# Down projection of a gated MLP by Strassen's scheme in seven of its eight groups, on one core

## Chip, cores and metric

The kernel runs on one core of a Trainium2 chip. The metric is device time in microseconds (us) for one launch, the median of the runs shown. TensorE is written PE, its weight loads PEld, VectorE DVE, ScalarE ACT, GpSimd POOL, and SyncE, which issues the transfers, SP.

## What is computed

One layer of a decoder trunk on 512 tokens of width 1024 in float32. A mixing stage (four token mixers, gates, an output projection) gives a residual `h`; then comes an MLP with a norm on both sides. The change touches only the MLP and where its buffers lie:

```python
h = h + rms_norm(mix, norm_mix_post[l])
u = rms_norm(h, norm_mlp_pre[l])
hid = jnp.square(jax.nn.relu(jnp.einsum("btd,df->btf", u, w_up[l])))   # 1024 -> 4096
m = jnp.einsum("btf,fd->btd", hid, w_down[l])                          # 4096 -> 1024
h = h + rms_norm(m, norm_mlp_post[l])
```

## The kernel before

**Three matmuls for one.** Every float32 operand x is split into a high part, a rounded copy that ACT writes (L140), and a low part, x minus the high part, that DVE writes (L141). A product is then three matmuls, high by high, high by low and low by high, issued by `mm3` (L181 to L183), each with a moving operand of 512 columns. A weight unit is 128x1024: `load` brings it into one of three `raw` buffers (L135, on SP), `prep` splits it into one of six pairs `whi`, `wlo`, and `unit` hands units out in the order of use, preparing four ahead.

**The MLP.** The 4096 hidden features are done in 8 groups (`NG`) of 512, that is 4 blocks (`GF`) of 128. `up_group` makes the hidden values of a group in two pairs of blocks: a pair is 48 matmuls (2 blocks, 8 blocks of the inner width, 3 products) into two PSUM banks of 512, and `up_out` then applies relu on ACT (L850), a square on DVE (L851) and the split. The first group, `up_first`, runs in two column halves of 256, so that it can start when only half the tokens are normalised; the last two token tiles are transposed between (L807). `down_group` multiplies: for each of 4 token tiles and each half of the 1024 outputs, 12 matmuls of 512 columns (4 blocks, 3 products) into one PSUM bank, added to the sum `macc` in SBUF by DVE (L914; in group 0 ACT copies it, L912). So a group is 96 matmuls up and 96 down. The order is up 0, up 1, down 0, up 2, down 1 and so on. In the last group every finished row of tokens is squared and summed on ACT (L738), scaled by the gain (L888), multiplied by its norm factor and added to the residual `h1`, which stayed in SBUF (L892), and stored (L894).

A down group's core:

```python
 904            for pi, (a, b) in enumerate(pieces):
 905                ps = sm_bank()[:, : b - a]
 906                for j in range(GF):
 907                    wh, wl = us[j]
 908                    mm3(ps, hh[j // 2][:, j % 2, t * P : t * P + P], hl[j // 2][:, j % 2, t * P : t * P + P],
 909                        wh[:, a:b], wl[:, a:b], j == 0, j == GF - 1)
 910                m = macc[t][:, a:b]
 911                if g == 0:
 912                    act.activation(m, ps, AF.Copy)
 913                    continue
 914                dve.tensor_tensor(m, m, ps, ALU.add)
```

**What sets the order.** The program is written as above; a scheduler with its own estimate of durations places the instructions on each engine, so on PE the matmuls of an up pair and of a down group can be interleaved. Each engine then runs its list strictly in order, and waits for the others at semaphores. Buffers of a pool are reused in turn, so a write to a buffer waits for its last reader.

Of the kernel before, what the change touches and what calls it, by code (L numbers as in the profile page):

```python
# [49 lines left out]
def tile_hybrid_trunk(ctx: ExitStack, tc: tile.TileContext, xT, xn, wts, par, bd, cst, msk, gains, out):  # L50
# [5 lines left out]
    yp = ctx.enter_context(tc.tile_pool(name="yp", bufs=8))  # L56
    ap_ = ctx.enter_context(tc.tile_pool(name="ap", bufs=4))
    tp = ctx.enter_context(tc.tile_pool(name="tp", bufs=10))
# [3 lines left out]
    mp = ctx.enter_context(tc.tile_pool(name="mp", bufs=4, space=bass.MemoryType.PSUM))  # L62
    qp = ctx.enter_context(tc.tile_pool(name="qp", bufs=4, space=bass.MemoryType.PSUM))
    npool = ctx.enter_context(tc.tile_pool(name="np", bufs=2))

# [33 lines left out]
    bd_h = cp.tile([P, 6, P], F32R, name="bd_h")  # L99
    bd_l = cp.tile([P, 6, P], F32R, name="bd_l")  # L100
    msk_s = cp.tile([P, len(MASKED), 64], U8, name="msk_s")
    rstd_bc = cp.tile([P, T], F32, name="rstd_bc")
    sbd = cp.tile([P, 3, 2, P], F32, name="sbd")
# [14 lines left out]

    NU = wts.shape[0]
# [23 lines left out]
    def prep(n):  # L143
        while Wt.n_prep < min(n, NU):
            i = Wt.n_prep
# [17 lines left out]
            Wt.hl[i] = (hi, lo)  # L163
            Wt.n_prep += 1
            load(i + 3)

# [88 lines left out]
    ssq = cp.tile([P, NT], F32, name="ssq")  # L255
# [91 lines left out]
    lbt = cp.tile([P, 8], F32, name="lbt")  # L347
# [35 lines left out]
    vz = cp.tile([P, NT, 2, 192], F32, name="vz")  # L383
# [42 lines left out]
    def lru_steps():  # L426
# [28 lines left out]
        spt = cp.tile([P, 16], F32, name="spt")  # L455
# [49 lines left out]
    def hgrn_steps():  # L505
# [39 lines left out]
        ds_ = cp.tile([P, 4 * NT], F32, name="ds_")  # L545
# [84 lines left out]
        ms = cp.tile([P, 16], F32, name="ms")  # L630
        rs = cp.tile([P, 16], F32, name="rs")
# [83 lines left out]
    load_gain(1)  # L715
    h1 = []
# [117 lines left out]

    def up_mm(bk, w, h, a, b):
        wh, wl = w
        for kk in range(4):
            k = 4 * h + kk
            for c in range(2):
                o = kk * W + c * P  # L840
                mm3(bk[c][:, a:b], wh[:, o : o + P], wl[:, o : o + P],
                    U(u2h, k, a, b), U(u2l, k, a, b), k == 0, k == NK - 1)

    def hid_tiles():
        return [[yp.tile([P, 2, T], F32R, tag="y", name=nm("hid")) for _ in range(2)] for _ in range(2)]

    def up_out(hid, s, bk):
# [6 lines left out]
    def up_first():  # L854
        hid = hid_tiles()
        bks = [[mm_bank(), mm_bank()] for _ in range(2)]
        us = {}
        for h in range(2):
            for s in range(2):
                us[s, h] = unit()  # L860
                up_mm(bks[s], us[s, h], h, 0, 256)
                if (s, h) in ((1, 0), (0, 1)):
                    t = 2 if h == 0 else 3
                    tb = trans(t, sm_bank)
                    put(t, 0, tb[0])
                    put(t, 1, tb[1])
        for s in range(2):
            for h in range(2):
                up_mm(bks[s], us[s, h], h, 256, T)
            up_out(hid, s, bks[s])  # L870
        return hid

    def up_group():
        hid = hid_tiles()
        for s in range(2):
            bk = [mm_bank(), mm_bank()]
            for h in range(2):
                up_mm(bk, unit(), h, 0, T)
            up_out(hid, s, bk)
        return hid  # L880

    load_gain(2)
    macc = [ap_.tile([P, D], F32, tag="acc", name=nm("macc")) for _ in range(NT)]

    mgs = {}

    def gain(t, a, b):
        dve.tensor_tensor(mgs[t][:, a:b], macc[t][:, a:b], gbc[2][:, a:b], ALU.mult)  # L888

    def half(t, r, a, b):  # L890
        m = mgs[t][:, a:b]
        dve.scalar_tensor_tensor(m, m, r, h1[t][:, a:b], ALU.mult, ALU.add)  # L892
        eng = nc.scalar if t == NT - 1 and a == T else nc.sync
        eng.dma_start(out[t * P : t * P + P, a:b], m)  # L894

    def down_group(g, hid):
        hh, hl = hid
        us = [unit() for _ in range(GF)]
        last = g == NG - 1
        for t in range(NT):  # L900
            pieces = ((0, T), (T, 2 * T))
            if last and t == NT - 1:
                pieces = ((0, T), (T, T + 256), (T + 256, D))
            for pi, (a, b) in enumerate(pieces):
                ps = sm_bank()[:, : b - a]
                for j in range(GF):
                    wh, wl = us[j]
                    mm3(ps, hh[j // 2][:, j % 2, t * P : t * P + P], hl[j // 2][:, j % 2, t * P : t * P + P],
                        wh[:, a:b], wl[:, a:b], j == 0, j == GF - 1)
                m = macc[t][:, a:b]  # L910
                if g == 0:
                    act.activation(m, ps, AF.Copy)  # L912
                    continue
                dve.tensor_tensor(m, m, ps, ALU.add)  # L914
                if last:
                    sq_only(m, 4 + t, pi)
                    if pi < 1 or t < NT - 1:
                        v = sq_tot(4 + t, pi, stat[:, t, 6:7] if pi == 0 else v, 3 + pi)
                    if pi == 0:
                        mgs[t] = t_tile()[:, :D]  # L920
                    if t < NT - 1 or pi < 2:
                        gain(t, a, b)
            if last:
                if t == NT - 1:
                    v = sq_tot(4 + t, 1, v, 4)
                    v = sq_tot(4 + t, 2, v, 5)
                r = row_rstd(v, 4 + t, (lambda: gain(t, T + 256, D)) if t == NT - 1 else None)
                if t == NT - 1:
                    half(t, r, 0, T)
                    half(t, r, T, T + 256)  # L930
                    half(t, r, T + 256, D)
                else:
                    for a, b in ((0, T), (T, D)):
                        half(t, r, a, b)

    ahead[0] = 2
    hid = up_first()
    ahead[0] = 4
    for t in range(NT):
        row_eps(t)  # L940
    for g in range(1, NG):
        nh = up_group()
        down_group(g - 1, hid)
        hid = nh
    down_group(NG - 1, hid)


def _layout(inp):
# [38 lines left out]
    for g in range(1, NG + 1):  # L987
        if g < NG:
            upg(g)
        for j in range(GF):  # L990
            units.append(wd[GF * (g - 1) + j])
    wts = np.stack(units)

# [34 lines left out]
    return [xt, xn, wts, par, bd, cst, msk, gains]  # L1028
# [21 lines left out]
```

## Time and profile before

| | |
|---|---|
| median of 3 runs | 768.71 us (768.24 to 768.71) |
| the profiled execution | 768.58 us, of which its span 766.8 us |
| PE busy | 756.9 us, 99% of the span |
| DVE busy | 448.0 us, 58% |
| ACT busy | 262.8 us, 34% |
| TensorE's granted clock, mean | 0.998 of full speed |
| moved | 80.40 MB, mean 105 GB/s |

Times in the trace count from the span's start. A busy share is an average over stages; the MLP runs from 407 us to the end. A matmul's recorded duration is longer than its share of the engine, since matmuls overlap; the distance from start to start is what one costs.

### The profile page before, as it was taken

The numbers are of one execution on the slowest core, as the hardware profiler recorded it, in microseconds if no ns is written. First come the engines' busy times: TensorE is split into PE (matmuls) and PEld (weight loads), VectorE is DVE, ScalarE is ACT, GpSimd is POOL, SyncE is SP. The second block draws the span as 40 slices with busy tenths as digits, with TensorE's granted clock in tenths as the row PEclk, the third lists the DMA queues.
The fourth block names the chain that finished last, engine by engine and source line by source line (L and its number), as shares of the span: only waits on it lengthen the run. The fifth ranks groups of instructions, "written<-read, shape, count | busy, mean of one in ns | idle before, by whom it ended". The sixth has DMA issues, their size and how long they took to land.

```text
span 766.8 us, 8992 instructions
## 1 busy us (share of the span) xinstructions
PE 756.9 (99%) x3592; PEld 636.0 (83%) x3592; DVE 448.0 (58%) x709; ACT 262.8 (34%) x372; POOL 6.3 (1%) x11
## 2 busy tenths in 40 slices
PE   8999999999999999999999999999999999999995
PEld 7888988888888888888889988888888888888885
DVE  5798246559988476465476651445445453445347
ACT  6524122327323323333343743414132231314222
POOL 1100000000000000000000000000000000000000
PEclk9999999999999999999999999999999999999999
DMA  8632322132221362224312331404142230515002
GB/s 330 253 119 102 91 102 97 69 107 85 83 82 56 110 220 96 96 83 135 112 60 78 111 110 29 164 28 164 56 138 82 83 126 17 180 35 161 32 1 109
DMA packets 23945, 80.40 MB, mean 105 GB/s; under 512 B 2784, under 2 KB 3552, under 8 KB 23904
## 3 DMA queue, kind: packets, MB, share of 16 engines
q1 hardware_dynamic: 23616, 79.67, 31.0%
q8 instruction: 28, 0.46, 0.2%
q10 hardware_dynamic: 288, 0.17, 0.1%
q14 instruction: 13, 0.11, 0.0%
HBM read 77.73 MB, written 2.10 MB: 104 GB/s over the span
## 4 chain that ended last, share of the span: by engine, by line
PE 97%; DMA 1%; DVE 1%; SPq 0%; issue 0%; ACT 0%; DVEq 0%
PE mm L182 22%; PE mm L183 22%; PE mm L181 22%; PE sm L183 9%; PE sm L182 9%; PE sm L181 9%; PE sm L512 2%; DMA raw<-in_wts_dram 1%; PE sm L621 0%; PE sm L807 0%; DVE t L892 0%; PE sm L537 0%; SPq L126 0%; PE sm L598 0%; PE sm L619 0%
## 5 line engine op out<-in xcount | busy, mean ns | idle before, releaser
L140 ACT ACTIVATE whi<-raw 128x1024 fp32r<-128x1024 f32 (+1 forms) x132 | 136.8, 1046 | 333.0 <-PE mm L182 134.2
L141 DVE TENSOR_TENSOR wlo<-raw,whi 128x1024 fp32r<-128x1024 f32 (+1 forms) x132 | 158.6, 1206 | 134.5 <-ACT whi L140 133.8
L182 PE MATMUL mm<-ul,whi 128*128 128x512 f32 x384 | 149.5, 391 | 0.6 <-DVE ul L215 0.6
L181 PE MATMUL mm<-uh,whi 128*128 128x512 f32 x384 | 148.9, 393 | 0.5 <-ACT whi L140 0.5
L183 PE MATMUL mm<-uh,wlo 128*128 128x512 f32 x384 | 149.1, 390 | 0.0
L182 PE MATMUL mm<-u2l,whi 128*128 128x512 f32 (+1 forms) x288 | 105.2, 366 | 0.0
L183 PE MATMUL mm<-u2h,wlo 128*128 128x512 f32 (+1 forms) x288 | 105.0, 365 | 0.0
L181 PE MATMUL mm<-u2h,whi 128*128 128x512 f32 (+1 forms) x288 | 104.4, 366 | 0.0
L182 PE MATMUL sm<-wlo,hid 128*128 128x512 f32 (+1 forms) x260 | 100.3, 386 | 0.0
L183 PE MATMUL sm<-whi,hid 128*128 128x512 f32 (+1 forms) x260 | 100.3, 386 | 0.0
L181 PE MATMUL sm<-whi,hid 128*128 128x512 f32 (+1 forms) x260 | 100.0, 386 | 0.0
L182 PEld LDWEIGHTS mm<-ul,whi 128*128 128x128 f32 x384 | 72.4, 188 | 16.0 <-DVE ul L215 1.2
L181 PEld LDWEIGHTS mm<-uh,whi 128*128 128x128 f32 x384 | 72.0, 189 | 16.1 <-ACT whi L140 1.3
L183 PEld LDWEIGHTS mm<-uh,wlo 128*128 128x128 f32 x384 | 72.1, 188 | 15.0
L914 DVE TENSOR_TENSOR macc<-macc,sm 128x512 f32<-128x512 f32 (+1 forms) x57 | 38.4, 675 | 72.1 <-PE sm L183 72.0
L182 PEld LDWEIGHTS mm<-u2l,whi 128*128 128x128 f32 x288 | 54.3, 189 | 8.9
L183 PEld LDWEIGHTS mm<-u2h,wlo 128*128 128x128 f32 x288 | 54.3, 189 | 8.7
L181 PEld LDWEIGHTS mm<-u2h,whi 128*128 128x128 f32 x288 | 54.0, 189 | 8.8
L182 PEld LDWEIGHTS sm<-wlo,hid 128*128 128x128 f32 x260 | 48.8, 188 | 9.9
L181 PEld LDWEIGHTS sm<-whi,hid 128*128 128x128 f32 x260 | 48.8, 188 | 9.9
L183 PEld LDWEIGHTS sm<-whi,hid 128*128 128x128 f32 x260 | 48.8, 188 | 9.7
L851 DVE TENSOR_TENSOR s<-s 128x512 f32<-128x512 f32 x32 | 22.0, 688 | 38.4 <-ACT s L850 38.4
(239 smaller groups left out, 772.8 us busy)
## 6 DMA issues: line engine op xcount, KB each, us to landing
raw<-in_wts_dram SPq DMA_DIRECT2D x131, 512.0 KB, 3.4
t<-in_xn_dram SPq DMA_DIRECT2D x8, 512.0 KB, 8.2
xt<-in_xt_dram SPq DMA_DIRECT2D x8, 256.0 KB, 5.7
out_dram<-t SPq DMA_DIRECT2D x7, 256.0 KB, 2.0
t<-in_gains_dram SPq DMA_DIRECT2D x3, 512.0 KB, 5.7
t<-in_bd_dram SPq DMA_DIRECT2D x1, 384.0 KB, 5.7
raw<-in_wts_dram SPq DMA_DIRECT2D x2, 128.0 KB, 3.8
raw<-in_wts_dram SPq DMA_DIRECT2D x1, 256.0 KB, 5.2
```

The source lines that it names most:

```text
L140: act.activation(hi, src, AF.Copy)
L141: dve.tensor_tensor(lo, src, hi.bitcast(F32), ALU.subtract)
L181: pe.matmul(ps, lh, rh, start=first, stop=False)
L182: pe.matmul(ps, lh, rl, start=False, stop=False)
L183: pe.matmul(ps, ll, rh, start=False, stop=last)
L512: pe.matmul(bk[ct][:, cs].rearrange("s (h n b) -> s h n b", h=2, b=B), kk_[:, ct, cs], qo, start=True, stop=True)
L851: dve.tensor_tensor(rl, rl, rl, ALU.mult)
L914: dve.tensor_tensor(m, m, ps, ALU.add)
```

## The change

For groups 0 to 6 the 512 tokens, 512 features and 1024 outputs of a group are each cut in two, A (hidden values) and B (weights) becoming 2 by 2 blocks. Strassen's scheme gets the four result blocks from seven products of sums of blocks (`ORDER` names their numbers, in order of issue) in place of eight products of blocks. A product is 256 tokens by 256 features by 512 outputs: 2 x 2 x 3 = 12 matmuls of 512 columns, into a PSUM tile of two banks.

- **Weights.** A group's four down units come as two transfers of 1 MB each (`load_ab`), and `form` makes seven operands of 128x1024 from them, four by sums on DVE (L205 to L216 of the new file), each split like a unit.
- **Hidden values.** `up_out` runs on a whole pair: relu and square (now ACT) on 128x1024, three sums on DVE (L929 to L931), and splits of seven forms of 128x256 in place of four.
- **Sums.** Seven running sums `macc` of 128x1024, one for each product, one DVE addition each per group (L991). After group 6 seven DVE operations (`combine`) turn them into the four result blocks. Group 7 is done as before, and adds to these.
- **Order.** Up pairs run one pair further ahead: pairs 0, 1, 2, down 0, pairs 3 and 4, down 1, and so on; pair 15 follows down 6.
- **Space.** The new buffers lie over the mixing stage's, which are released in the MLP's first group. So `h1` is stored to DRAM (2 MB, `h1d`) and read back before the last group; the gain row is loaded late too. PSUM is two tiles of two banks for up and two for down.

In the diff, `split` is the function that puts L140 and L141 (now L159 and L160) in the lists; `mm3` is now L239 to L241, L807 is now L948 for token tiles 2 and 3.

```diff
+    ORDER = (1, 7, 5, 6, 4, 2, 3)
+    FORM = {1: 0, 2: 1, 4: 2, 7: 3, 5: 4, 6: 5, 3: 6}
...
+    def load_ab(g, x):
+        if g < NG - 1:
+            r = fp_.tile([P, 2, D], F32, tag="ab", name=nm("ab"))
+            nc.sync.dma_start(r, dn[g, x])
+            ab[g, x] = r
+
+    def form(g, n):
+        p = ORDER[n]
+        a, b = ab[g, 0], ab[g, 1]
+        if n == 0:
+            load_ab(g + 1, 0)
+            x = xp.tile([P, 2, T], F32, tag="x", name=nm("x"))
+            dve.tensor_tensor(x, a[:, :, T:], b[:, :, T:], ALU.add)
+            ab[g, 7] = x
+        if n == 1:
+            x = xp.tile([P, 2, T], F32, tag="x", name=nm("x"))
+            dve.tensor_tensor(x, a[:, :, :T], a[:, :, T:], ALU.add)
+            ab[g, 5] = ab[g, 6] = ab[g, 4] = x
...
+        hi = wp.tile([P, D], F32R, tag="whi", name=nm("fhi"))
+        lo = wp.tile([P, D], F32R, tag="wlo", name=nm("flo"))
...
-        for c in range(2):
-            rl = s_tile()
-            act.activation(rl, bk[c], AF.Relu)
-            dve.tensor_tensor(rl, rl, rl, ALU.mult)
-            split(hid[0][s][:, c], hid[1][s][:, c], rl)
+        q = hp.tile([P, 2, T], F32, tag="h", name=nm("q"))
+        act.activation(q, bk, AF.Relu)
+        act.activation(q, q, AF.Square)
...
+            dve.tensor_tensor(s[:, 0:2], b[:, 0::3], b[:, 1:2].to_broadcast([P, 2, HT]), ALU.subtract)
+            dve.tensor_tensor(s[:, 2], b[:, 0], s[:, 1], ALU.add)
+            dve.tensor_tensor(s[:, 3], s[:, 2], b[:, 2], ALU.subtract)
+            split(hi[:, 0], lo[:, 0], b[:, 0])
+            split(hi[:, 1:3], lo[:, 1:3], b[:, 2:4])
+            split(hi[:, 3:], lo[:, 3:], s)
...
+    def down_group(g):
+        aa = (hid.pop(2 * g), hid.pop(2 * g + 1))
+        for p in ORDER:
+            wh, wl = unit()
+            ps = dn_bank()
+            f = FORM[p]
+            for tt in range(2):
+                o = tt * P
+                for j in range(2):
+                    ah, al = aa[j]
+                    mm3(ps[:, tt], ah[:, f, o : o + P], al[:, f, o : o + P],
+                        wh[:, j * T : j * T + T], wl[:, j * T : j * T + T], j == 0, j == 1)
+            if g == 0:
+                macc[p] = ma.tile([P, 2, T], F32, tag="ma", name=nm("macc"))
+                act.activation(macc[p], ps, AF.Copy)
+            else:
+                dve.tensor_tensor(macc[p], macc[p], ps, ALU.add)
...
+    up_pair(2)
+    for g in range(NG - 1):
+        down_group(g)
+        if g < NG - 2:
+            up_pair(2 * g + 3)
+            up_pair(2 * g + 4)
+        else:
+            combine()
+            up_pair(2 * g + 3)
```

**Where the order moves: PE at the start of the MLP.** `sm_3103` (now `sm_3112`) is the mixing stage's last product, `mm_3170` (now `ub_3178`) the first up bank, `t_2962` token tile 2 before its transpose, `u2h` and `u2l` the split normalised tokens. Before:

```order
L183 MATMUL sm_3103<-sp_2899,ylo_2779 128x512
L181 MATMUL mm_3170<-u2h_3099,whi_2933 128x256 [waits Activation_49]
L181 MATMUL mm_3171<-u2h_3099,whi_2933 128x256
L807 MATMUL sm_3222<-ident,t_2962 128x128 [waits DVE_49]
L807 MATMUL sm_3222<-ident,t_2962 128x128 x3
L807 MATMUL sm_3227<-ident,t_2962 128x128 [waits PE_49]
L807 MATMUL sm_3227<-ident,t_2962 128x128 x3
L182 MATMUL mm_3170<-u2l_3100,whi_2933 128x256 [waits DVE_49]
```

and now:

```order
L241 MATMUL sm_3112<-sp_2905,ylo_2784 128x512
L239 MATMUL ub_3178<-u2h_3108,whi_2939 128x256 [waits DVE_49]
L240 MATMUL ub_3178<-u2l_3109,whi_2939 128x256
L241 MATMUL ub_3178<-u2h_3108,wlo_2940 128x256
L239 MATMUL ub_3178<-u2h_3108,whi_2939 128x256
```

The eight transposes stood between the products that need only `u2h` and the first that needs `u2l`; now they come 48 matmuls later, and the first product waits for DVE.

**DVE while a down group runs.** Before, a group's first additions, with little between them:

```order
L914 TENSOR_TENSOR macc_3162<-macc_3162,sm_4502 128x512 [waits PE_49]
L141 TENSOR_TENSOR hid_4333<-s_4473,hid_4331 128x512 [waits Activation_49]
L914 TENSOR_TENSOR macc_3162<-macc_3162,sm_4516 128x512 [waits PE_49]
L914 TENSOR_TENSOR macc_3163<-macc_3163,sm_4530 128x512 [waits PE_49]
L914 TENSOR_TENSOR macc_3163<-macc_3163,sm_4544 128x512 [waits PE_49]
```

and now, group 2, from the operand of product 2 (`flo_4215`) over the addition of product 1 (`macc_3611`) to that of product 7 (`macc_3631`); `flo_4233` is the operand of product 3, `alo` and `s` belong to the up pair that has just ended:

```order
L160 TENSOR_TENSOR flo_4215<-ab_3843,fhi_4214 128x1024 [waits PE_49,Activation_49]
L991 TENSOR_TENSOR macc_3611<-macc_3611,db_4181 128x1024 [waits PE_49]
L929 TENSOR_TENSOR s_630_4166<-q_4161 128x512 [waits Activation_49]
L160 TENSOR_TENSOR flo_4233<-ab_3843,fhi_4232 128x1024 [waits Activation_49]
L160 TENSOR_TENSOR alo_4165<-q_4161,ahi_4164 128x256 [waits Activation_49]
L930 TENSOR_TENSOR s_630_4166<-q_4161,s_630_4166 128x256 [waits DVE_49]
L160 TENSOR_TENSOR alo_4165<-q_4161,ahi_4164 128x512 [waits Activation_49]
L991 TENSOR_TENSOR macc_3631<-macc_3631,db_4200 128x1024 [waits PE_49]
```

Six operations now stand between the first two additions' ends, and PE's product 6, the fourth of the group, waits for the second addition, since it reuses that PSUM tile. On PE, products 1, 7 and 5 stand back to back and only two matmuls of an up pair come before product 6.

**DVE at the end.** `macc_3165` is the sum of the last token tile, `t_5583` the output row of the tile before it; L749 (now L808) adds up a norm, L888 (now L1029) is the gain, L892 (now L1033) the output, L914 (now L1051) the addition. Before, around the last addition:

```order
L749 SCALAR_TENSOR_TENSOR stat<-stat 128x1 [waits Activation_49]
L763 SCALAR_TENSOR_TENSOR stat<-nt_5605,stat 128x1 [waits DVE_49]
L914 TENSOR_TENSOR macc_3165<-macc_3165,sm_5651 128x256 [waits PE_49]
L892 SCALAR_TENSOR_TENSOR t_5583<-t_5583,stat,t_2801 128x512 [waits DVE_49]
L892 SCALAR_TENSOR_TENSOR t_5583<-t_5583,stat,t_2801 128x512
L888 TENSOR_TENSOR t_5632<-macc_3165,t_3160 128x256 [waits DVE_49]
L749 SCALAR_TENSOR_TENSOR stat<-stat 128x1 [waits Activation_49]
```

and now, from the last tile's first half (`macc_3690`) on; `macc_3650` holds the second halves of the last two tiles:

```order
L1051 TENSOR_TENSOR macc_3690<-macc_3690,db_5677 128x512 [waits PE_49]
L1029 TENSOR_TENSOR mg_5695<-macc_3690,g_851_5527 128x512 [waits DVE_49]
L1051 TENSOR_TENSOR macc_3650<-macc_3650,db_5629 128x512 [waits PE_49]
L1029 TENSOR_TENSOR mg_5646<-macc_3650,g_851_5527 128x512 [waits DVE_49]
L1051 TENSOR_TENSOR macc_3650<-macc_3650,db_5677 128x256 [waits PE_49]
L808 SCALAR_TENSOR_TENSOR stat<-stat 128x1 [waits Activation_49]
L1029 TENSOR_TENSOR mg_5695<-macc_3650,g_851_5527 128x256 [waits DVE_49]
L817 TENSOR_SCALAR nh_5666<-stat 128x1 [waits DVE_49]
L808 SCALAR_TENSOR_TENSOR stat<-stat 128x1 [waits Activation_49]
```

Before, one addition and one gain follow the last matmul for the last tile; now the addition of the tile before it, its gain and its norm stand around the last tile's own, and both tiles' outputs come after them. PE's last product waits for the first row shown, which empties its PSUM tile.

## Rows read from the trace of the kernel before

**Rows 1.** Page: span, busy time and share of each engine, granted clock by slice.

```profile
span 766.8 us, 8992 instructions
PE 756.9 (99%) x3592; PEld 636.0 (83%) x3592; DVE 448.0 (58%) x709; ACT 262.8 (34%) x372; POOL 6.3 (1%) x11
...
PEclk9999999999999999999999999999999999999999
```

**Rows 2.** Page: the chain that ended last, by engine.

```profile
PE 97%; DMA 1%; DVE 1%; SPq 0%; issue 0%; ACT 0%; DVEq 0%
```

**Rows 3.** Busy time (and instructions) by stretch: PE, PEld, DVE, ACT, POOL; clock, DMA share, GB/s.

```profile
407.40:757.40 350.00, 350.00 (x1649) 294.22 (x1648) 166.75 (x242) 112.19 (x170) 0.00 (x0) 1.00 0.27 89
...
560.00:600.00 40.00, 40.00 (x178) 33.14 (x177) 19.33 (x23) 12.54 (x16) 0.00 (x0) 1.00 0.31 106
```

**Rows 4.** Timeline of the MLP: start, duration, engine, instruction, idle before and releaser.

```profile
559.93 0.39 PE L183 MATMUL sm<-whi,hid 128*128 128x512 f32 x1
...
560.35 0.69 DVE L914 TENSOR_TENSOR macc<-macc,sm 128x512 f32<-128x512 f32 x1 [2.04 <-PE sm L183]
...
579.65 0.39 PE L183 MATMUL mm<-u2h,wlo 128*128 128x512 f32 x1
```

**Rows 5.** DVE by line, 480 to 700 us: count, busy us, mean ns, idle before.

```profile
L141 DVE TENSOR_TENSOR wlo<-raw,whi 128x1024 fp32r<-128x1024 f32 x41 | 49.7, 1223 | 37.1 <-ACT whi L140 37.1
L914 DVE TENSOR_TENSOR macc<-macc,sm 128x512 f32<-128x512 f32 x40 | 27.4, 685 | 55.3 <-PE sm L183 55.3
L851 DVE TENSOR_TENSOR s<-s 128x512 f32<-128x512 f32 x20 | 13.8, 688 | 26.8 <-ACT s L850 26.8
```

**Rows 6.** DVE by line, 470 to 767 us: the 256-column addition.

```profile
L914 DVE TENSOR_TENSOR macc<-macc,sm 128x256 f32<-128x256 f32 x2 | 0.8, 422 | 0.1
```

**Rows 7.** ACT by line, 480 to 700 us.

```profile
L140 ACT ACTIVATE whi<-raw 128x1024 fp32r<-128x1024 f32 x42 | 43.5, 1057 | 116.5 <-PE sm L183 81.5 <-DMA raw<-in_wts_dram 25.5 <-PE mm L182 7.4
L140 ACT ACTIVATE hid<-s 128x512 fp32r<-128x512 f32 x20 | 12.6, 628 | 8.9 <-DVE s L851 8.9
L850 ACT ACTIVATE s<-mm 128x512 f32<-128x512 f32 x20 | 11.8, 590 | 33.1 <-PE mm L183 33.1
```

**Rows 8.** Timeline of DVE, 600 to 645 us: operations that follow without a wait.

```profile
605.65 1.23 DVE L141 TENSOR_TENSOR wlo<-raw,whi 128x1024 fp32r<-128x1024 f32 x1 [1.09 <-ACT whi L140]
606.79 0.68 DVE L914 TENSOR_TENSOR macc<-macc,sm 128x512 f32<-128x512 f32 x1
...
630.41 0.68 DVE L851 TENSOR_TENSOR s<-s 128x512 f32<-128x512 f32 x1
631.02 0.68 DVE L141 TENSOR_TENSOR hid<-s,hid 128x512 fp32r<-128x512 f32 x1
```

**Rows 9.** Timeline at the start of the MLP, PE and DVE.

```profile
407.41 0.40 PE L181 MATMUL mm<-u2h,whi 128*128 128x256 f32 x2
...
407.65 1.03 PE L807 MATMUL sm<-ident,t 128*128 128x128 f32 x8
...
408.54 0.39 PE L182 MATMUL mm<-u2l,whi 128*128 128x256 f32 x1
...
409.00 0.68 DVE L141 TENSOR_TENSOR u2l<-mm,u2h 128x512 fp32r<-128x512 f32 x1
```

**Rows 10.** Page, transfers: count, KB each, median us from issue to landing.

```profile
raw<-in_wts_dram SPq DMA_DIRECT2D x131, 512.0 KB, 3.4
```

**Rows 11.** Timeline of the end.

```profile
757.43 0.28 PE L181 MATMUL sm<-whi,hid 128*128 128x256 f32 x1
...
758.75 0.28 PE L183 MATMUL sm<-whi,hid 128*128 128x256 f32 x1
...
759.06 0.42 DVE L914 TENSOR_TENSOR macc<-macc,sm 128x256 f32<-128x256 f32 x1
...
762.13 1.54 DVE L892 SCALAR_TENSOR_TENSOR t<-t,stat,t 128x512 f32<-128x512 f32 x3
```

More of the change, by code (lines that the diff above doesn't have):

```diff
@@ L49, in tile_hybrid_trunk @@
 @with_exitstack
-def tile_hybrid_trunk(ctx: ExitStack, tc: tile.TileContext, xT, xn, wts, par, bd, cst, msk, gains, out):
+def tile_hybrid_trunk(ctx: ExitStack, tc: tile.TileContext, xT, xn, wts, dn, par, bd, cst, msk, gains, out):
     nc = tc.nc
@@ L117, in tile_hybrid_trunk, with more_units @@
         hl = {}
+    ORDER = (1, 7, 5, 6, 4, 2, 3)
+    FORM = {1: 0, 2: 1, 4: 2, 7: 3, 5: 4, 6: 5, 3: 6}
+    NMIX = 68
+    items = [("u", i) for i in range(NMIX)]
+    def more_units(n):
+        m = sum(1 for x_ in items if x_[0] == "u")
+        items.extend(("u", m + i) for i in range(n))
+    more_units(6)
+    for g in range(NG - 1):
+        items.extend(("f", g, n) for n in range(7))
+        more_units(4 if g < NG - 2 else 2)
+    more_units(GF)
+    NI = len(items)
     NU = wts.shape[0]
@@ L143, in prep @@
     def prep(n):
[L144 to L145 removed]
+        while Wt.n_prep < min(n, NI):
+            item = Wt.n_prep
+            if items[item][0] == "f":
+                Wt.hl[item] = form(*items[item][1:])
+                Wt.n_prep += 1
+                continue
+            i = items[item][1]
             load(i + 1)
@@ L715, in tile_hybrid_trunk @@
     load_gain(1)
+    h1d = dp.tile([T, D], F32, name="h1d")
     h1 = []
@@ L873, in up_group @@
[L873 to L934, printed above, removed]
@@ new lines, in tile_hybrid_trunk @@
+    bks = [up_bank(), up_bank()]
+    us = {}
+    ahead[0] = 2
+    for h in range(2):
+        for s in range(2):
+            us[s, h] = unit()
+            up_mm(bks[s], us[s, h], h, 0, 256)
+            if (s, h) in ((1, 0), (0, 1)):
+                t = 2 if h == 0 else 3
+                tb = dn_bank()
+                for k in range(NK):
+                    pe.transpose(tb[:, k // 4, (k % 4) * P : (k % 4) * P + P], u2[t][:, k * P : k * P + P], ident)
+                for j in range(2):
+                    put(t, j, tb[:, j].rearrange("p (k t) -> p k t", k=4))
@@ L940, in tile_hybrid_trunk, with up_pair @@
         row_eps(t)
[L941 to L945, printed above, removed]
+    def up_pair(pair):
+        bk = up_bank()
+        for h in range(2):
+            up_mm(bk, unit(), h, 0, T)
+        up_out(pair, bk)
+    macc = {}
+    def down_group(g):
[6 more added lines that the diff above has]
+                o = tt * P
+                for j in range(2):
+                    ah, al = aa[j]
[6 more added lines that the diff above has]
+                dve.tensor_tensor(macc[p], macc[p], ps, ALU.add)
@@ new lines, in combine, with tt, cm @@
+    def combine():
+        def tt(o, x, y, op):
+            dve.tensor_tensor(macc[o], macc[x], macc[y], op)
+        tt(6, 6, 1, ALU.subtract)
+        tt(1, 1, 2, ALU.add)
+        tt(2, 6, 5, ALU.subtract)
+        tt(3, 2, 3, ALU.subtract)
+        tt(7, 6, 7, ALU.subtract)
+        tt(4, 4, 7, ALU.subtract)
+        tt(5, 7, 5, ALU.subtract)
+    def cm(t, a, b):
+        p = ((1, 3), (4, 5))[t // 2][a // T]
+        return macc[p][:, t % 2, a % T : a % T + b - a]
+    up_pair(2)
+    for g in range(NG - 1):
+        down_group(g)
+        if g < NG - 2:
+            up_pair(2 * g + 3)
+            up_pair(2 * g + 4)
+        else:
+            combine()
+            up_pair(2 * g + 3)
@@ new lines, in tile_hybrid_trunk, with gain, half @@
+    hr = []
+    for i in range(2):
+        r = fp_.tile([P, 2, D], F32, tag="ab", name=nm("hr"))
+        nc.sync.dma_start(r, h1d[2 * i * P : 2 * i * P + 2 * P, :].rearrange("(t p) d -> p t d", p=P))
+        hr.append(r)
+    g2 = xp.tile([P, D], F32, tag="x", name=nm("g2"))
+    nc.sync.dma_start(g2, gains[2:3, :].to_broadcast([P, D]))
+    mgs = {}
+    def gain(t, a, b):
+        dve.tensor_tensor(mgs[t][:, a:b], cm(t, a, b), g2[:, a:b], ALU.mult)
+    def half(t, r, a, b):
+        m = mgs[t][:, a:b]
+        dve.scalar_tensor_tensor(m, m, r, hr[t // 2][:, t % 2, a:b], ALU.mult, ALU.add)
+        eng = nc.scalar if t == NT - 1 and a == T else nc.sync
+        eng.dma_start(out[t * P : t * P + P, a:b], m)
@@ L986, in _layout @@
     upg(0)
[L987 to L991, printed above, removed]
+    for g in range(1, NG):
+        upg(g)
+    for j in range(GF):
+        units.append(wd[GF * (NG - 1) + j])
     wts = np.stack(units)
+    dn = wd.reshape(NG, 2, 2, P, D)[: NG - 1].transpose(0, 2, 3, 1, 4)
     def cols(v):
```

145 lines of the change are left out of this document (101 added, 44 removed).

## Prediction, made before the changed kernel was run

> **What bounds the kernel now.** Read the page's busy shares first: PE is busy 99% of the span at full granted clock, DVE 58%, ACT 34% [rows 1]. A busy PE need not be the limit, so the chain that ended last comes next: 97% of it is PE [rows 2]. Then the stage that the change touches: from 407.4 to 757.4 us PE has no idle time at all, while DVE works 167 of 350 us [rows 3]. So in the MLP one matmul less is worth one matmul's distance, as long as PE waits for nothing new. That distance is read from starts: from 559.93 to 579.65 us lie 87 matmuls of 512 columns, 0.2267 us each, though each is recorded with 0.39 us [rows 4]. The question for the change is whether DVE, which gets most of the new work, is still in time.
>
> **What goes.** Each of seven groups has 84 down matmuls in place of 96: 7 x 12 = 84 fewer, and the lists of PE agree. 84 x 0.2267 = **19.0 us less**. The Trainium skill (TensorE: Matmul & The Clock Gate, section Back-to-back issue gap) gives 215.7 ns for such a matmul alone, by which it would be 18.1 us; the trace's 226.7 decides.
>
> **What a group costs DVE and ACT.** A group takes PE 180 x 0.2267 = 40.8 us instead of 43.5. DVE has 24 operations of 128x1024 in it (11 weight splits, 4 weight sums, 7 additions into `macc`, 2 hidden splits), 4 of 512, 6 of 256. The 1024s are priced by the weight split, 1.223 us [rows 5]; an addition from PSUM of 1024 columns does not occur, but 512 columns cost 0.685 from PSUM and 0.688 from SBUF [rows 5], and 256 cost 0.422 [rows 6], so 1024 make 0.685 + 2 x 0.263 = 1.21: the same. The sum is 24 x 1.223 + 4 x 0.688 + 6 x 0.422 = 34.6 us. Operations that wait for nothing start closer together than they last, 1.14 us after a 1024 and 0.61 after a 512 [rows 8]; with 0.34 for a 256 (estimate, 0.422 less the same 0.08) it is 31.8 us. So DVE goes from 19.3 of 40 us [rows 3] to 78 to 85% of 40.8 us: no bound, but little air. ACT has 11 splits of 1.057, and per pair a relu (0.590 + 0.43 = 1.02 for 1024), a square of 1.06 and splits of 0.41 (estimate, by the slope from 1024 to 512), 0.63 and 1.06: 11.6 + 8.4 = 20.0 us of 40.8 [rows 7], half its time.
>
> **Inside a group** the tightest place is product 6, the fourth on PE. Count from the group's first matmul. Products 1, 7 and 5 and two up matmuls end at 38 x 0.2267 = 8.6 us; product 6 reuses product 7's PSUM tile, so its addition must be over. DVE starts product 1's addition 0.42 us after the start of its last matmul [rows 4], at 2.9 us, and then has, before product 7's, a 512, a 1024, two 256 and a 512. By distances product 7's addition starts at 2.9 + 1.14 + 0.61 + 1.14 + 0.34 + 0.34 + 0.61 = 7.1 and ends at 8.3: in time by 0.3. By full durations it ends at 2.9 + 1.22 + 0.69 + 1.22 + 0.42 + 0.42 + 0.69 + 1.22 = 8.8, late by 0.2. The addition before it can itself be late: the operand of product 2, ahead of it on DVE, waits for an ACT split whose buffer is freed by the last up matmul of the group before; that split ends at 0.2 + 1.06 = 1.3 and the operand at 2.5, in time by 0.4. Six groups have this place (group 0 is added by ACT): 0 to 0.5 us each, 0 to 3 in all; I take **+0.5**, near the distances, since they are what the trace shows for such sequences.
>
> **The start of the MLP.** Before, the eight transposes of tile 2 (from 407.65 us) fill PE until `u2l` is ready and the first product with it starts at 408.54 [rows 9]. Now they come 48 matmuls later and the first product waits for DVE from 407.41: +1.1 us. If it waits for the third of the `u2l` writes (409.00 + 0.68 [rows 9]) it is 2.3; were it none, 0. The product reads only what the first of them (407.80 in the old list, before 408.54) writes: **+1.1**. The transposes themselves are not saved or added.
>
> **The first Strassen group.** Its weights overlie the mixing stage and can load only when the last `h1` is stored, some 418 us; 1 MB lands in 3.4 to 6.8 us (512 KB take 3.4 [rows 10]), say at 425. Then DVE has 12 operations of 1024, 4 of 512 and 6 of 256 before the last operand of product 7: 12 x 1.223 + 4 x 0.688 + 6 x 0.422 = 20 us, to 445. PE wants it after 192 half products of 0.12 us (distance in [rows 11]) and 16 transposes of 0.11 [rows 9], 48 matmuls and 16 more: 408.5 + 23.0 + 1.8 + 10.9 + 3.6 = 447.8. The cover is 3 us, and DVE waits for ACT on the way: 0 to 3, I take **+0.3**. Behind the 1 MB loads on SP stand only weight units that are needed later; 2 MB more to DRAM and back is work for transfer engines that are busy 0.27 of the time [rows 3], and costs nothing.
>
> **The end.** Pair 15 now comes directly before group 7, which needs it at once. From its last matmul to its low part: 0.2 + 1.02 + 1.06 + 1.06 + 1.22 = 4.6 us. PE fills it with 16 matmuls of 512 and 8 of 256 of group 7, 3.6 + 1.0 = 4.6: **+0.3** (0 to 1). `combine`, seven operations, 8 us, lies on DVE between additions in a stretch where PE does 42 up matmuls, and ends before its result is wanted. In group 7 each two-bank tile is emptied half by half by DVE, which also has gains, norms and outputs of earlier tiles: counted along its list, the addition that frees the last product's tile ends 0.6 us late: **+0.6** (0 to 1.5). After it, before, DVE's last output ended 762.13 + 1.54 - 757.43 = 6.2 us from the last product's start [rows 11]. Now its list holds one more addition (0.69), two more gains (1.38), and nearly all of the norm of tile 2, with ACT's squares of three pieces in line before it; counted through, 8.1 us: **+1.9** (0.5 to 2.5, the lower end if the outputs overlap the norm as before).
>
> **Sum.** -19.0 + 0.5 + 1.1 + 0.3 + 0.3 + 0.6 + 1.9 = -14.3. Against the profiled execution of 768.58 us (its span 766.8; the median of the runs is 768.71, the same within 0.02%) that is **754.3 us**. With all low ends -18.5, or 750.1; with all high ends -5.7, or 762.9.
>
> **Rivals.** *DVE paces the groups.* The orders leave 0.3 to 0.4 us at two places in each group; if operations with operands in three dimensions, or those that wait for their predecessor on DVE, cost what is recorded and not the distance, product 6 is late by 0.5 us in each of six groups; with 1 us late, 6 us: 757 to 760. For it: 85% load in strict order. Against: [rows 8]. The Trainium skill (VectorE: DVE Perf Modes, section The DRAIN you can't avoid) says that the next operation does not start until the pipeline is empty, which is this case; the rows with 0.61 us from start to start of 0.68 us speak against it here. *The two-bank additions run at half pace, 2.4 us, since no row shows one.* Then two of them before product 6 make it 9.1 + 2.4 - 8.6 = 2.9 us late in six groups, 17 us: **771 us, slower than before**. It decides from about 2.3 us per addition. Against: 256 and 512 columns from PSUM cost as from SBUF. *The matmuls aren't saved*, for instance since the smaller products cost more each: their shapes are 128x512 as before, so this has almost nothing for it; the waits alone would remain, 768.6 + 4.7 = 773 us.
>
> **How the numbers follow.** The forecast, with PE nearly gapless, 0.72 (750.5 to 757.5); DVE paces, 0.20 (757.5 to 764); half pace, 0.05; not saved, 0.03. Two in ten are left out by 750.5 to 761.5. The measurement tells 0.2% (1.5 us) from no change: faster 0.92, same 0.02, slower 0.06.
>
> **What would show it.** Right: 84 matmuls fewer at 0.2267 us; DVE 75 to 85% busy from 450 to 730 us; PE idle for about 1 us near 408 us and under 0.5 us in front of each product 6; `macc` additions of 1024 near 1.21 us; DVE's last output about 8 us after the last product's start. Wrong: waits of PE for `macc` or for operands of over 1 us in every group; additions over 2 us; a stall at the first product 7 of more than 3 us; or a clock below full in any stretch of the MLP.

## The result, and the profile after

The changed kernel takes 758.58 us (median of four runs, 758.39 to 758.70) against 768.64 us of the kernel before, measured beside it: a ratio of 0.987, 95% interval 0.9853 to 0.9887, 10.1 us or 1.3% faster. The forecast was 754.3 us in a range of 750.5 to 761.5. So the sign and the range hold, and 4.3 us of the 14.3 forecast are missing. The profiled execution took 758.39 us, its span 756.6.

The page of the changed kernel, to be held against [rows 1]: 84 matmuls fewer, DVE 90 us busier, ACT 50, the clock full in every slice.

```profile
span 756.6 us, 8896 instructions
...
PE 745.2 (98%) x3508; PEld 620.4 (82%) x3508; DVE 538.5 (71%) x781; ACT 313.0 (41%) x404; POOL 6.4 (1%) x11
...
PEclk9999999999999999999999999999999999999999
```

Busy time by stretch, columns as in [rows 3]:

```profile
407.40:440.00 32.60, 31.74 (x241) 30.24 (x240) 24.34 (x57) 19.86 (x39) 0.00 (x0) 1.00 0.50 192
440.00:720.00 280.00, 280.00 (x1218) 228.86 (x1217) 214.59 (x223) 135.21 (x147) 0.00 (x0) 1.00 0.29 98
560.00:600.00 40.00, 40.00 (x175) 32.67 (x175) 31.62 (x34) 19.06 (x21) 0.00 (x0) 1.00 0.31 105
```

DVE is busy 31.6 of 40 us, 79%, as forecast (78 to 85%), and ACT 19.1 of 40 (20.0 of 40.8 forecast). PE has no idle time from 440 to 720 us. Yet it gets through 175 matmuls in 40 us where it did 178 [rows 3]. That is the first sign that the missing time is not a wait.

PE's waits in the whole program (total us, times, longest us):

```profile
PE sm L282 <- DVE spt L525: 1.0, 1, 1.0
PE ub L239 <- DVE u2l L160: 0.9, 1, 0.9
PE mm L240 <- DVE ul L273: 0.6, 1, 0.6
PE mm L239 <- ACT uh L270: 0.2, 1, 0.2
```

Only the second lies in the MLP, at its start. There is none for `macc`, for a Strassen operand, for pair 15 or for the last product's tile. These rows miss short waits: idle time counts from the recorded end of the matmul before, 0.39 us after its start, while its share is 0.227, so each wait costs some 0.16 us more than its row says, and one shorter than that has no row. By starts, only two distances between 512-column matmuls of the MLP are over 0.245 us, those behind 728.79 and 730.03 us, just after the splits of pair 15 end:

```profile
728.79 0.47 PE L239 MATMUL db<-whi,ahi 128*128 128x512 f32 x1
729.10 0.39 PE L240 MATMUL db<-wlo,ahi 128*128 128x512 f32 x1
...
730.03 0.49 PE L241 MATMUL db<-whi,alo 128*128 128x512 f32 x1
730.36 0.40 PE L239 MATMUL db<-whi,ahi 128*128 128x512 f32 x1
```

They hold 0.2 us between them. DVE by line, 480 to 700 us, has the addition that no row before showed (count, busy us, mean ns, idle before):

```profile
L991 DVE TENSOR_TENSOR macc<-macc,db 128x1024 f32<-128x1024 f32 x36 | 43.9, 1218 | 24.1 <-PE db L241 24.1
```

It takes 1.218 us; 1.21 was the estimate. Then the start of the MLP in the timeline, for [rows 9], and the end, for [rows 11]:

```profile
409.23 0.40 PE L241 MATMUL sm<-sp,ylo 128*128 128x512 f32 x1
...
409.76 0.68 DVE L160 TENSOR_TENSOR u2l<-mm,u2h 128x512 fp32r<-128x512 f32 x1
...
410.49 0.39 PE L239 MATMUL ub<-u2h,whi 128*128 128x256 f32 x1 [0.86 <-DVE u2l L160]
...
746.40 0.28 PE L239 MATMUL db<-whi,ahi 128*128 128x256 f32 x1
...
751.90 1.54 DVE L1033 SCALAR_TENSOR_TENSOR mg<-mg,stat,hr 128x512 f32<-128x512 f32 x3
```

Before, the mixing stage's last matmul stood right in front of the MLP's first, at 407.41 [rows 9]:

```profile
407.19 0.39 PE L183 MATMUL sm<-sp,ylo 128*128 128x512 f32 x1
```

From the one to the other it is 0.22 us before and 1.26 after (409.23 to 410.49): PE's wait costs 1.0 us. DVE's last output ends 751.90 + 1.54 - 746.40 = 7.0 us after the last product's start (6.2 before, 8.1 forecast). But the last matmul of the mixing stage, whose products the change leaves alone, starts at 409.23 us and not at 407.19. Some 2 us are lost before the MLP begins.

**Where they go.** Take three products that follow each other without a gap, 36 matmuls of 512 columns, in the changed kernel's timeline:

```profile
611.92 0.40 PE L239 MATMUL db<-fhi,ahi 128*128 128x512 f32 x1
...
620.05 0.40 PE L241 MATMUL db<-fhi,alo 128*128 128x512 f32 x1
```

8.13 us for 35 distances are 232.3 ns each, not the 226.7 of [rows 4]. Sorted by the tiles that they read, the distances from one 512-column matmul to the next (those above 300 ns left out) have these means:

| moving, stationary operand | count | before, ns | after, ns |
|---|---|---|---|
| mixing input `u`, weights | 1123 | 227.1 | 227.2 |
| MLP input `u2`, weights (up) | 672 | 226.7 | 227.8 |
| branch outputs `y`, weights (mixing) | 185 | 227.4 | 232.5 |
| weights, branch outputs `y` (mixing) | 143 | 226.8 | 233.2 |
| hidden values: down products | 755 before, 665 after | 226.7 | 232.7 |

What is slow reads a `y` tile or a hidden form, in the mixing stage too, whose matmuls are the same as before and only lie elsewhere in SBUF. Those two kinds share a place: the forms lie over the `y` tiles. The sizes of the pools in the two kernels give how far behind the first `u` buffer each kind starts (bytes per partition, and their rest by 256):

| | `u`, `u2` | weights | `y` and hidden |
|---|---|---|---|
| before | 0 (0) | 142592 (0) | 32768 (0) |
| after | 0 (0) | 51200 (0) | 100736 (128) |

All offsets inside the operands of 512-column products are multiples of 256 bytes. Before, all three kinds have the same rest; now the six 64-byte buffers of the small norm pool follow the weights, and the `y` tiles start behind these 384 bytes. Theory A: the rest of the distance between a matmul's two operands sets its pace. The trace of before held a case of it that the prediction did not look at, twelve gate products of the mixing stage whose stationary tile `bd_h` or `bd_l` lies, counted in the same way, at a rest of 32 and whose moving tiles lie at 0 or 128. Its timeline:

```profile
140.68 0.40 PE L181 MATMUL sm<-t,bd_h 128*128 128x512 f32 x1
...
143.26 0.39 PE L183 MATMUL sm<-t,bd_l 128*128 128x512 f32 x1
```

2.58 us for 11 distances, 234.5 ns. The rival, theory B, is the prediction's own: DVE paces the groups, for which it gave 757 to 760 us, and the time measured lies there. Theory C is that the region of SBUF matters.

### The profile page after: what moved, and what is told of

It is laid out like the page before. It is cut to its first block, busy times and chain, and to the rows that moved or that the text cites. A ratio compares the mean times of both kernels' runs of the same rounds, so it can differ in the third digit from the quotient of the medians.

```text
span 756.6 us, 8896 instructions
## 1 busy us (share of the span) xinstructions
PE 745.2 (98%) x3508; PEld 620.4 (82%) x3508; DVE 538.5 (71%) x781; ACT 313.0 (41%) x404; POOL 6.4 (1%) x11
## 4 chain that ended last, share of the span: by engine, by line
PE 96%; DVE 2%; DMA 1%; issue 1%; SPq 0%; ACT 0%; DVEq 0%; ACTq 0%
PE mm L240 15%; PE mm L241 15%; PE mm L239 15%; PE ub L241 8%; PE ub L239 8%; PE ub L240 8%; PE db L239 7%; PE db L241 7%; PE db L240 7%; PE sm L570 2%; PE sm L239 1%; PE sm L240 1%; PE sm L241 1%; DMA raw<-in_wts_dram 1%; PE sm L679 0%
## 5 line engine op out<-in xcount | busy, mean ns | idle before, releaser
L159 ACT ACTIVATE whi<-raw 128x1024 fp32r<-128x1024 f32 (+2 forms) x104 | 108.6, 1044 | 255.1 <-PE mm L240 124.5
L160 DVE TENSOR_TENSOR wlo<-raw,whi 128x1024 fp32r<-128x1024 f32 (+2 forms) x104 | 124.9, 1201 | 75.7 <-ACT whi L159 75.3
L241 PE MATMUL mm<-uh,wlo 128*128 128x512 f32 x384 | 149.1, 390 | 0.0
L239 PE MATMUL mm<-uh,whi 128*128 128x512 f32 x384 | 148.8, 393 | 0.2 <-ACT uh L270 0.2
L239 PE MATMUL ub<-u2h,whi 128*128 128x512 f32 (+1 forms) x288 | 105.5, 367 | 0.9 <-DVE u2l L160 0.9
L241 PE MATMUL ub<-u2h,wlo 128*128 128x512 f32 (+1 forms) x288 | 105.6, 367 | 0.0
L240 PE MATMUL ub<-u2l,whi 128*128 128x512 f32 (+1 forms) x288 | 105.4, 366 | 0.0
L239 PEld LDWEIGHTS mm<-uh,whi 128*128 128x128 f32 x384 | 72.0, 188 | 16.0 <-ACT whi L159 0.7
L241 PEld LDWEIGHTS mm<-uh,wlo 128*128 128x128 f32 x384 | 72.1, 188 | 15.0
L239 PE MATMUL db<-fhi,ahi 128*128 128x512 f32 x196 | 77.5, 395 | 0.0
L240 PE MATMUL db<-flo,ahi 128*128 128x512 f32 x196 | 77.4, 395 | 0.0
L241 PE MATMUL db<-fhi,alo 128*128 128x512 f32 x196 | 77.3, 394 | 0.0
L991 DVE TENSOR_TENSOR macc<-macc,db 128x1024 f32<-128x1024 f32 x42 | 51.2, 1218 | 26.1 <-PE db L241 26.1
L239 PEld LDWEIGHTS ub<-u2h,whi 128*128 128x128 f32 x288 | 54.3, 189 | 10.3 <-DVE u2l L160 1.3
L240 PEld LDWEIGHTS ub<-u2l,whi 128*128 128x128 f32 x288 | 54.3, 189 | 9.1
L241 PEld LDWEIGHTS ub<-u2h,wlo 128*128 128x128 f32 x288 | 54.3, 189 | 8.9
L159 ACT ACTIVATE fhi<-x 128x1024 fp32r<-128x1024 f32 x28 | 29.6, 1058 | 39.2 <-PE db L241 27.5
L241 PEld LDWEIGHTS db<-fhi,alo 128*128 128x128 f32 x196 | 37.0, 189 | 8.7
L239 PEld LDWEIGHTS db<-fhi,ahi 128*128 128x128 f32 x196 | 36.9, 188 | 8.5
```

The lines of the kernel that those rows point to most:

```text
L159: act.activation(hi, src, AF.Copy)
L160: dve.tensor_tensor(lo, src, hi.bitcast(F32), ALU.subtract)
L991: dve.tensor_tensor(macc[p], macc[p], ps, ALU.add)
```

## The experiments

### 128 bytes in front of the overlaid tiles

```diff
+    pad = ctx.enter_context(tc.tile_pool(name="pad", bufs=1))
+    pad.tile([P, 32], F32, name="pad_t")
     mix = ctx.enter_context(ExitStack())
```

> The changed kernel with 128 bytes per partition left free ahead of the mixing stage's tiles, so that these tiles, and the hidden forms laid over them, start at a multiple of 256 bytes as the weight tiles do. Nothing else differs. Theory A (a 512-column matmul takes 226.8 ns from start to start where its two operands' addresses differ by a multiple of 256 bytes, and 232.6 where not; 1068 of the changed kernel's are of the second kind, 20 of the kernel before's): 1056 of these 1068 become of the first kind, 1056 x 5.8 ns = 6.1 us less, 752.4 us, MLP starts 2.2 us earlier. Theory B (DVE paces the groups, which is why the change fell 4.3 us short of the forecast): DVE's work is the same, so 758.6 us. Theory C (the tiles are slow because of the region of SBUF in which they now lie): 128 bytes change nothing, 758.6 us.

Measured: 751.22 us, ratio 0.9776 (0.9761 to 0.979) to the kernel before: 7.4 us less than the change alone. Its timeline has the same 36 matmuls (lines are two further on) in 7.94 us, 226.9 ns each; over all 588 of them the mean is 226.7.

```profile
607.40 0.39 PE L241 MATMUL db<-fhi,ahi 128*128 128x512 f32 x1
...
615.34 0.39 PE L243 MATMUL db<-fhi,alo 128*128 128x512 f32 x1
```

The 1056 matmuls are 5.8 ns faster than in the change alone, which is 6.2 us; the up products, 672, are 1.1 ns faster too, 0.7 us, though their own operands keep their rest. The spans differ by 6.8 us. B and C fall: DVE has the same operations to do, and the region is the same but for 128 bytes. Once more, beside another kernel:

> The kernel with the 128-byte gap alone once more, on the same chip as the one with other banks, to compare them: 751.2 us, 0.9775 of the time before.

Measured: 751.30 us, 0.9777 (0.9763 to 0.979).

### 256 bytes, and 128 bytes in the kernel before

The control is the same edit with `[P, 64]`:

> The changed kernel with 256 bytes per partition left free in the same place, the control for the 128: every tile behind it moves, and all distances modulo 256 stay as they were. Theory A: 758.6 us, matmuls on the hidden forms still at 232.6 ns. Were it the moving of tiles as such that helps, or where one of them ends, it would be as fast as with 128 bytes, 752.4 us.

Measured: 758.66 us, 0.9872 (0.9858 to 0.9887), the down products at 232.7 ns. Moving alone does nothing. In the kernel before the gap goes in front of the weights' pool:

```diff
+    pad = ctx.enter_context(tc.tile_pool(name="pad", bufs=1))
+    pad.tile([P, 32], F32, name="pad_t")
     wp = ctx.enter_context(tc.tile_pool(name="wp", bufs=6))
```

> The kernel before with 128 bytes per partition left free ahead of its weight tiles alone, so that 2964 of its 512-column matmuls have operands whose addresses differ by 128 modulo 256 (20 had before). Theory A: 2964 x 5.8 ns = 17.2 us slower, 785.8 us, at full granted clock and with no new wait of PE. Theory B: DVE is far from bounding the kernel before, so 768.6 us. Theory C: the weights move by 128 bytes in the same region, 768.6 us.

Measured: 784.69 us, 1.0207 (1.019 to 1.0224), 16.2 us slower for 2964 more matmuls with unlike rests, 5.5 ns each. The busy time by stretch has its MLP, PE without idle time and the clock full, and the timeline 40 down matmuls in a row:

```profile
422.00:774.00 352.00, 352.00 (x1601) 289.26 (x1600) 161.10 (x231) 109.91 (x165) 0.00 (x0) 1.00 0.25 86
```

```profile
598.91 0.39 PE L184 MATMUL sm<-wlo,hid 128*128 128x512 f32 x1
...
607.98 0.40 PE L184 MATMUL sm<-wlo,hid 128*128 128x512 f32 x1
```

9.07 us for 39 distances, 232.6 ns. So 128 bytes make the kernel before 2% slower with no instruction changed, and no wait or busy share shows it.

### 64 and 192 bytes

`[P, 16]` and `[P, 48]` in place of `[P, 32]`.

> The changed kernel with 64 bytes per partition left free ahead of the mixing stage's tiles: the operands' addresses of the 1056 matmuls then differ by 64 or 192 modulo 256 where it was 128. Theory A in the form that only multiples of 256 are free of cost: 758.6 us, as the change without a gap. If the price goes with the distance, something between 752.4 and 758.6 us, or above. Theories B and C: 758.6 us.

Measured: 754.77 us, 0.9821 (0.9806 to 0.9836): between the two, so "any unlike rest costs the same" falls. The down products stand at 228.9 ns, but the mixing products with `y` as moving operand, whose distance has the other sign, at 233.3. So the sign was tried:

> The changed kernel with 192 bytes left free ahead of the mixing stage's tiles. With 64 bytes, matmuls whose moving operand lies 64 bytes behind the stationary one modulo 256 took 228.9 ns, those with 192 bytes 233.3 ns; 864 of the first kind (hidden forms, and branch outputs as stationary operands), 192 of the second (branch outputs as moving operands). With 192 bytes the two change places. If the signed distance, moving less stationary, modulo 256 sets the price: 864 at 233.3 ns and 192 at 228.9, so 864 x 6.5 + 192 x 2.2 ns = 6.0 us over the 751.2 us of the aligned kernel, 757.2 us. If it is the kind of tile that sets it (hidden forms cheap, branch outputs as moving operands dear) or the unsigned distance: as with 64 bytes, 754.8 us.

Measured: 758.31 us, 0.9872 (0.9855 to 0.9888), 1.1 us over the sum of theory A; the up products are at 227.8 ns again, which is 0.7 of it. The down products are at 233.2 ns, the mixing products with `y` moving at 229.8: the kinds have changed places. The 36 matmuls in the timelines with 64 and with 192 bytes:

```profile
609.90 0.39 PE L241 MATMUL db<-fhi,ahi 128*128 128x512 f32 x1
...
617.91 0.39 PE L243 MATMUL db<-fhi,alo 128*128 128x512 f32 x1
```

```profile
611.87 0.40 PE L241 MATMUL db<-fhi,ahi 128*128 128x512 f32 x1
...
620.04 0.39 PE L243 MATMUL db<-fhi,alo 128*128 128x512 f32 x1
```

### One and two DVE operations more per group

The rest is run on the kernel with 128 bytes, called aligned. How near is product 6 to waiting? Its timeline has, in one group, the addition of product 7, the two DVE operations after it, and the first matmul of product 6:

```profile
573.67 1.21 DVE L993 TENSOR_TENSOR macc<-macc,db 128x1024 f32<-128x1024 f32 x1
...
574.80 0.42 DVE L933 TENSOR_TENSOR s<-s,q 128x256 f32<-128x256 f32 x1
...
575.14 1.22 DVE L162 TENSOR_TENSOR wlo<-raw,whi 128x1024 fp32r<-128x1024 f32 x1
...
575.22 0.39 PE L241 MATMUL db<-fhi,ahi 128*128 128x512 f32 x1
```

Product 7's addition ends at 573.67 + 1.21 = 574.88: 0.3 us of air.

```diff
                 dve.tensor_tensor(macc[p], macc[p], ps, ALU.add)
+                if p == 1:
+                    for _ in range(1):
+                        dve.tensor_tensor(scr, macc[1], macc[1], ALU.add)
```

> The changed kernel with the 128-byte gap (751.2 us), and in each of six groups one addition of 128x1024 more on DVE, 1.22 us, which lands between the addition of product 1 and that of product 7; PE's order in the groups stays the same. In the trace with the gap product 7's addition starts at 573.67 us and ends, by distances, at 574.8, while product 6, which waits for it, starts at 575.13: 0.3 us of air, as the prediction counted. Theory P (the tight place is product 6, with 0.3 us of air, and the prediction's 0.5 us per group was merely the wrong end): product 6 comes 1.14 - 0.3 = 0.8 us late in each of six groups, some 5 us, 756 us, with PE waiting for the addition into macc six times. Theory S (DVE has slack of more than one operation there, and the prediction's term had no ground at all): 751.2 us and no wait.

Measured: 756.72 us, 0.9846 (0.9833 to 0.986), 5.5 us more, and PE's waits have a new row:

```profile
PE db L241 <- DVE macc L994: 3.5, 5, 0.7
```

Theory P: one operation too many, and product 6 waits in five of the six groups. The row holds 3.5 us. Set beside the aligned trace, matmul by matmul from the MLP's first on, product 6 starts 0.86 us later in each of the five (0.70 of the row and the 0.16 that a row leaves out) and the matmul after it another 0.11: 4.9 of the 5.4 us by which this MLP is longer. In the sixth group the two make 0.2 us and no row. With `range(2)`:

> The same with two operations more per group; the second lands behind product 7's addition, and the up matmuls between products 6, 4 and 2 are dealt out a little differently. DVE's load goes from 31.8 to 34.1 us of 40.8 per group. If only the place ahead of product 6 counts: as with one operation more, 756 us. If DVE's load as such paces the groups (the rival): twice the loss of one operation, some 761 us.

Measured: 756.77 us, 0.9849 (0.9834 to 0.9865), with the same row of PE's waits, 3.5 us in 5. The second operation is free. It is the place ahead of product 6 that counts, and DVE's load as such does not pace the groups.

### The saved matmuls put back

```diff
-                for j in range(2):
+                for j in (0, 1) * (2 if p == 3 else 1):
```

> The changed kernel with the 128-byte gap, and product 3 of every Strassen group accumulated twice: 84 matmuls of 512 columns more, as many as the change saved, and nothing else. The text's output is then not the reference's: product 3 enters it doubled. If a matmul saved is worth one distance: 84 x 0.2267 = 19.0 us more, 770.3 us, so that all the rest of the change, DVE's work, the order and the end, costs 770.3 - 768.5 = 1.8 us. If the change had hidden costs that its longer waits cover, the sum is less: for each us that PE waits now and could fill, one us less.

(This expectation is wrong in one point: the second round begins the sum anew, so product 3 enters once and not doubled.) Measured: 770.44 us, 1.0027 (1.0016 to 1.0037). Over 751.30 that is 19.1 us for 84 matmuls, 228 ns each: what the change saved is worth its distance, and all the rest of it costs 770.44 - 768.46 = 2.0 us when the operands are aligned.

### The start of the MLP

```diff
+    late_trans(2, bks[1])
     for h in range(2):
         for s in range(2):
             us[s, h] = unit()
             up_mm(bks[s], us[s, h], h, 0, 256)
```

(`late_trans` holds the eight transposes and their split, which stood in the loop.)

> The changed kernel with the 128-byte gap, and the eight transposes of tile 2 ahead of the first up product, into the PSUM tile that the second up product will use. In the trace with the gap PE waits 0.94 us for u2l there, the only wait of the MLP. If that wait is what the moved transposes cost (the prediction's +1.1 us): 0.9 us less, 750.3 us, and no wait of over 0.2 us at the start of the MLP. If the first product then waits for something else (the PSUM tile that the transposes fill, or the later tiles' chain on DVE): 751.2 us or above, with a wait of another name.

Measured: 752.03 us, 0.9785 (0.9772 to 0.9799): no gain. Run again for its profile:

> The kernel with the 128-byte gap and the transposes of tile 2 in front once more, for its profile; its runs were at 752.0 us, not the 750.3 expected. Either the 0.94 us wait for u2l is gone and PE waits that much or more at another place near 408 us, or the wait is gone and PE's pace has changed elsewhere. 751.5 to 752.5 us again; the wait that stands in the trace decides.

Measured: 752.09 us, 0.9791 (0.9776 to 0.9805). PE's waits:

```profile
PE ub L944 <- DVE u2l L162: 1.0, 1, 1.0
...
PE ub L241 <- DVE stat L810: 0.2, 1, 0.2
```

The wait now stands at the transposes (L944), which read no `u2l` at all. Nor does the matmul that waits in the changed kernel at 410.49 us, `ub<-u2h,whi`, 0.05 us after that DVE operation ends (409.76 + 0.68). What the two have in common is that they write a two-bank PSUM tile of the MLP, which lies over banks of the mixing stage; and the operation waited for, `u2l<-mm`, reads transposes of tile 1 from such a bank. Which bank lies under which tile no trace shows. So the transposes got two banks that nobody reads any more, and the pools changed places:

```diff
+    tb2 = trans(2, mm_bank)
     mixps.close()
-    bp = ctx.enter_context(...)
-    dq = ctx.enter_context(...)
+    dq = ctx.enter_context(...)
+    bp = ctx.enter_context(...)
```

> The kernel with the 128-byte gap; the transposes of tile 2 are issued ahead of the first up product into two single PSUM banks of the mixing stage that nobody reads any more, and the two PSUM pools of the MLP change places, so that the first up product's tile no longer lies over a bank that holds transposes of tile 1. In the run with the transposes in front the 0.95 us wait only moved onto the transposes, since their tile lay over that bank too. Theory T (the wait at the start of the MLP is for the PSUM bank, and for the first u2l at the same time, and the transposes fill it when they have banks of their own): PE without a wait of over 0.2 us there, 0.9 us less than the kernel with the gap, 750.3 us. If the wait is for u2l alone and the transposes delay DVE's list by as much: 751.2 us or above with a wait for u2l.

Measured: 750.20 us, 0.9762 (0.9748 to 0.9775), 1.1 us under the aligned kernel of the same call (749.61 to 750.36 against 751.08 to 751.52). It is the fastest version, 18.2 us under the kernel before. Its timeline:

```profile
406.82 0.39 PE L243 MATMUL sm<-sp,ylo 128*128 128x512 f32 x1
407.05 1.04 PE L869 MATMUL mm<-ident,t 128*128 128x128 f32 x8
...
407.42 0.69 DVE L162 TENSOR_TENSOR u2l<-mm,u2h 128x512 fp32r<-128x512 f32 x1
...
407.85 0.36 PE L241 MATMUL ub<-u2h,whi 128*128 128x256 f32 x1
...
408.16 0.39 PE L242 MATMUL ub<-u2l,whi 128*128 128x256 f32 x1
```

The first up product starts at 407.85, while the DVE operation that it waited for in the changed kernel still runs (407.42 + 0.69 = 408.11). So it does not need that result, which leaves the bank. The first product with `u2l` starts when that result is there, at 408.16, and has no row among the waits.

## Why the prediction was right, and where its sum was off

The direction, the range and the mechanism of the saving hold (PE is the limit, and a matmul less is worth its distance); two groups of terms were off, in opposite directions. In us, against the profiled execution of before:

| step of the prediction | forecast | measured | from |
|---|---|---|---|
| 84 matmuls at 0.2267 | -19.0 | -19.1 | the 84 put back |
| pace of all other matmuls | 0, unsaid | +7.0 | 1056 x 6.0 ns, 672 x 1.1 ns over before |
| product 6 waits for `macc` | +0.5 | 0 | PE's waits and starts |
| start of the MLP | +1.1 | +1.0 | starts: 1.26 less 0.22 |
| first Strassen group | +0.3 | 0 | PE's waits and starts |
| pair 15 before group 7 | +0.3 | +0.2 | two long distances at 729 and 730 us |
| tile of the last product | +0.6 | 0 | PE's waits |
| the end | +1.9 | +0.8 | 7.0 less 6.2 |
| sum | -14.3 | -10.1 | spans: -10.2 |

**The step that failed** is "A group takes PE 180 x 0.2267 = 40.8 us": the distance of [rows 4] was carried over to matmuls whose operands the change had moved. From product 6 of one group to product 6 of the next, 180 matmuls, it is 41.4 us in the changed kernel and 40.8 in the aligned one. The prediction took the buffers laid over the mixing stage's as a matter of transfers and reuse, and costed a new address at nothing. With the addresses put right the kernel is at 751.2 us, so the term is 7.4 us by the medians.

**The stall terms** were 4.7 us in sum and are 2.0. Where the prediction counted by distances it was exact: product 6 has 0.3 us of air, as it said, and the price of too much DVE work there appears with one operation more. It was wrong to take 0.5 us at the place all the same, as a hedge. At the start of the MLP the price was right and the reason only half: the first up product waits for a PSUM bank before the next one could wait for `u2l`. The end was counted 1.1 us too long. That the miss is 4.3 us and not 7, and that the range held, is partly luck: the stall terms were 2.7 us too high, and that hid as much of the pace.

**The rivals.** "DVE paces the groups" named 757 to 760 us, and the time fell there. It is nonetheless wrong: no row of PE's waits names `macc`, and 128 bytes take 7.4 us away with DVE's work unchanged. For it stood the Trainium skill (VectorE: DVE Perf Modes, section The DRAIN you can't avoid), by which the next operation does not start until the pipe is empty; the same section adds that a next operation that is not held starts earlier. The trace agrees with the addition: in the rows of the aligned kernel the next one starts 1.13 us after one of 1.21 (573.67, 574.80) and 0.34 after one of 0.42 (575.14). "Half pace" fell with 1218 ns, "not saved" with the 84 put back.

**What would show it** held in four of five points: 84 fewer, DVE's share, additions near 1.21 us, PE idle 0.9 us near 410 and not before product 6. The fifth, 8 us at the end, was 7. The list named 0.2267 us for the 84 alone and lacked what mattered, the distance of the matmuls that stay.

## What to carry to other kernels

When buffers move, compare the distances from start to start of unchanged matmuls before looking for waits: a slower pace shows as a busy engine. Keep the start addresses of all tiles that meet in a matmul alike modulo 256 bytes (shown here for float32r matmuls of 512 columns); small buffers (here 384 bytes of them) belong behind the large pools, not between. And a time that falls into a rival's range proves nothing of that rival until its wait is seen.

## What was not expected of the hardware

Pace of a 512-column float32r matmul in these runs, by (moving less stationary address) modulo 256:

| rest | ns | from |
|---|---|---|
| 0 | 226.7 | 755 before, 588 aligned |
| 64 | 228.9, 229.8 | 588 with 64 bytes, 185 with 192 bytes |
| 128 | 232.8, 232.3 | 588 of the change, 755 of before with 128 bytes |
| 192 | 233.2, 233.3 | 588 with 192 bytes, 185 with 64 bytes |

The Trainium skill (SBUF — State Buffer, section Who interferes with whom) gives PE two independent read ports, one for the moving operand and one for weights, and says that PE never waits on anyone; by that one would not look for a price of the rest. The runs differ by 6 ns per matmul, and the measurement decides. What in the chip causes it stays open.

The up products, whose own rest is 0, run at 227.8 ns in the changed kernel and at 226.7 in the aligned one. Sorted by their place, the excess lies next to slow matmuls alone: the first nine behind a down product take 229.5 ns (221 of them), the last one ahead of a down product 232.5 (17 more), and all others 226.7 (434). So the pace of a slow kind reaches over a change of kind by some nine matmuls; why was not tried, nor were other shapes and types.
